# Convolution layer: second weights of the first group and the table transfers put elsewhere

## The chip, the cores and the metric

The kernel runs on one core of a Trainium2 chip. The metric is the device time of one execution in microseconds; the time before is the median of three runs. The profiles are hardware traces of one execution. The engines are PE (matrix products; its weight loads are shown as PEld), DVE (vector operations), ACT (activations and copies), POOL (here almost only an issuer of DMA transfers, among them those that add to what lies at the destination) and SP (issues plain DMA transfers).

## The reference

A decoder trunk of two layers on 512 tokens of width 1024: first an attention layer with a gated MLP, then a convolution layer with a gated MLP. The change concerns the input projection of the convolution layer:

```python
def short_conv_mixer(h, norm_g, w_in, conv_w, w_out):
    xn = rms_norm(h, norm_g)
    proj = xn @ w_in
    gate_b = proj[..., :CONV_WIDTH]
    gate_c = proj[..., CONV_WIDTH:2 * CONV_WIDTH]
    u = proj[..., 2 * CONV_WIDTH:]
    y = gate_b * causal_dwconv(gate_c * u, conv_w)
    return y @ w_out
```

`rms_norm` scales each token by the reciprocal root of its mean square and each channel by a gain. The result is added to `h`, and an MLP follows (`conv_ffn`: up-projection, a convolution of width 3, a SiLU gate, down-projection).

## The kernel before

**Precision.** Each fp32 operand is split into a high and a low part (ACT writes the high part by a copy, L315 and L1029, DVE the rest by a subtraction, L316 and L1031), and a product is taken as three matmuls: high with high, low with high, high with low. Tiles are named accordingly: `whi_p2c` and `wlo_p2c` are the two parts of the weights for the product p2 of the convolution layer (the c at the end), `p_hic` and `p_loc` the parts of its activations.

**Seven products for eight.** The large projections are cut into 2 x 2 blocks (two halves of the width, two halves of the tokens) and computed with seven block products in place of eight, p1, p7, p3, p6, p2, q5 and q4 (class `Sevens`, function `seven`). One product is 24 matmuls of 128 x 256. For a group `g` of columns the weights arrive as blocks X, Y, W and Z by SP's loads; the sums that the products need are made in place: POOL adds a block into Y by a DMA, DVE adds X to Y (L1148, kept in the program as `up.summed`), POOL adds another block into X by a DMA (L1108), DVE adds W to Y (L1203). So p1 takes X, p7 takes Y, p6 takes Y with X added, p2 takes W, q5 takes X with a block added, q4 takes Y with W added, and p3 takes Z. `weights_of` splits one of them; `up.rest` is the low part that it made last. The buffers of the high and low parts rotate, three of each, and SP's loads into W, Z and the plain weights share three buffers as well.

**The convolution layer** (`conv_seven`). The first four tiles of the input projection are plain products (`accs`, 24 matmuls of 128 x 512 each) with the table `plan` that says what is issued at which step (tile, k). Meanwhile the sum of squares is finished, its reciprocal root is turned into a row over the tokens (`norm.row`, tile `nrow`), `row2` is the square of that row, and `gate(o)` scales one of the four tiles by the row and so frees its bank. Then 35 slots follow, seven for each of five groups 0 to 4; slot 7 g + s issues product s of the list above for group g (in place of p3 of the own group, that of the group before). Slot 5 of the last group takes its p3. In slot s == 2, `kept` copies p7's result (`P7s`) on ACT and the weights of p2 are split, if they have not been split before. After it comes the output projection with weights `in_conv_w_out` (L309 loads, split at L315 and L316), whose left operand is `y`, `y_hi` and `y_lo`.

**Tables.** The second MLP uses tables of summed weights (`t`, in device memory), made from `in_ffn_w_up` by DMA steps on POOL (`table_steps`, L114 and L117), each of which moves 768 KB or 1 MB from device memory to device memory. Most are issued during attention; the last seven, of the third table, are issued by `sum_far(99)` in slot 30 of the convolution layer (group 4, s == 2).

**Order.** The program is written in one order, and the framework puts each engine's instructions into a queue by that order and by what is ready in its model; an engine runs its queue in order. `pin` keeps an instruction in program order among the pinned ones of its engine (all of POOL's transfers, and the high parts in `weights_of`). `behind(a, b)` puts a behind b in their engine's queue. `norm.scaled(fn)` calls `fn` as soon as the row has been written in the program, which here is inside `spread`, directly behind the copy of the row on ACT (L397).

Of the kernel before, what the change touches and what calls it, by code (L numbers as in the profile page):

```python
# [17 lines left out]
F32 = mybir.dt.float32  # L18
# [4 lines left out]
ALU = mybir.AluOpType  # L23
AX = mybir.AxisListType

P = 128
# [31 lines left out]
def trunk(  # L58
# [17 lines left out]
    pin = tc.keep_in_program_order  # L76
    act, dve, pe, pool = InOrder(nc.scalar), InOrder(nc.vector), nc.tensor, nc.gpsimd
# [4 lines left out]
    tiny = ctx.enter_context(tc.tile_pool(name="tiny", bufs=4))  # L82
# [7 lines left out]
    def bank(tag):  # L90
        n_ps[0] += 1
        return ps.tile([P, S], F32, tag=tag, name=f"ps{tag}{n_ps[0]}", bufs={"a": 2, "b": 4, "c": 2}[tag])

    def f32(ap):
        return ap.bitcast(F32)
# [120 lines left out]
    def behind(later, earlier):  # L216

        tc.add_manual_dep(
            later.ins, earlier.ins.name,
            mybir.DependencyInfo(mybir.DependencyClass.NoSync, mybir.DependencyReason.DATA), reason="order",  # L220
        )
# [102 lines left out]
    def fetch(n):  # L324
        while len(ready) < min(len(wanted), at[0] + n):
            ready.append(load(len(ready)))
            split_all(len(ready) - 1)
# [209 lines left out]
    gate = const.tile([P, NB, 8], F32, tag="gate", name="gate")  # L537
# [328 lines left out]
    norm = Norm("n0", 0)  # L866
# [110 lines left out]
    def sum_far(n):  # L977
        for _ in range(n):
            next(sums_far, None)
# [26 lines left out]
    norm = Norm("n1", 0)  # L1006
# [365 lines left out]
    def conv_seven(norm, mp, rp):  # L1372
# [5 lines left out]
        up = Sevens("c", mp, range(5), block_of)  # L1378
# [7 lines left out]
        row2 = mp.tile([P, S], F32, tag="row2", name="row2")  # L1386
# [8 lines left out]
        def conv(o, src):  # L1395
            return causal_conv(place(o, 1)[:, 0, :], src, lambda i: conv_tap(i, o))
# [74 lines left out]
        def gate(o, acc):  # L1471
            return dve.tensor_tensor(early_b[:, o, :], acc, norm.row, op=ALU.mult)
# [8 lines left out]
        first = weights()  # L1481
        for f in (0, 1, 4, 5, 2, 3, 6, 7):
            raw.take(f)
        norm.scaled(lambda: dve.tensor_tensor(row2, norm.row, norm.row, op=ALU.mult))
        accs = [bank("b") for _ in range(4)]
        plan = {
            (0, 7): open_first, (1, 0): lambda: (raw.make("p7"), up.weights_of(0, "p1", "X")), (1, 2): lambda: raw.make("p6"),
            (2, 6): lambda: up.first_sums(0), (2, 7): lambda: (gate(0, accs[0]), gate(1, accs[1])), (3, 4): lambda: gate(2, accs[2])}
        for j, acc in enumerate(accs):
            for k, _ in enumerate(products(acc, weights() if j else first, (4, 5, 6, 7, 0, 1, 2, 3))):  # L1490
                if (j, k) in plan:
# [3 lines left out]
        for s in range(35):  # L1495
            up.slot(s // 7, s % 7)
            if s == 0:
                for to, src in zip(kept, up.forms["p1"]):
                    act.activation(to, f32(src), AF.Copy)
                up.forms["p1"] = kept  # L1500
                behind(gate(3, accs[3]), up.rest)
                behind(raw.make("q5"), up.summed)
            if s == 2:
                behind(raw.make("p3"), up.rest)
            if s == 30:
                sum_far(99)
            if s == 34:
                behind(conv(7, wides[3]["yg"][:, 1, :])[0], up.joined)
                fetch(1)
# [200 lines left out]
    with tc.tile_pool(name="mlp0", bufs=1, reuse_waits="tile") as mp:  # L1710
        norm = mlp(0, norm, mp)

    rp = ctx.enter_context(tc.tile_pool(name="rp", bufs=1))
    with tc.tile_pool(name="mix", bufs=1, reuse_waits="tile") as mp:
        ys, place = conv_seven(norm, mp, rp)

    with tc.tile_pool(name="mlp1", bufs=1, reuse_waits="tile") as mp:
        norm = Norm("n3", 8)
        blocks, up = up_begin(1, norm, mp, rp)
# [80 lines left out]
```

## Time and profile before

| What | Value |
|---|---|
| Median of three runs | 1120.63 us (1119.94 to 1121.14) |
| The profiled execution, its own time | 1119.98 us |
| Its span, first to last instruction | 1117.9 us |
| Granted clock of PE | 1.00 |
| Convolution layer, input projection in plain tiles | 609 to 633 us |
| Its five groups | 633 to 736 us |
| Output projection | 736 to 781 us |

A profile's page gives busy time by engine and the costliest groups. The views of the trace used below are: the timeline of one engine (start, duration, engine, line, operation, out<-in, shapes, and in brackets the idle time before it and what ended that), the chain of waits that ended last (start, duration, what), the waits of one engine (engine and line, who was waited for: us in total, times, longest), the DMA view of a window (queues: packets, MB, share of 16 DMA engines; issues: out<-in, KB each, us from issue to landing) and the groups by line. PE's matmuls are pipelined: a row lasts longer than the interval at which they are issued, so lost time on PE is best read from the starts.

### The profile page before, as it was taken

To read this page: it belongs to the slowest core of one execution; us is meant where nothing else is said; L and a number is where in the kernel's file an instruction comes from. 1 tells how busy PE (TensorE), PEld (TensorE's weight loads), DVE (VectorE), ACT (ScalarE), POOL (GpSimd) and SP (SyncE) were. 2 spreads that over 40 slices of the span, in tenths; PEclk is the share of its full clock that TensorE was granted. 3 is DMA by queue.
4 is the path that set the end of the run, shared out by engine and by line. 5 is a ranking of instruction groups with operands and counts; after the bars stand their busy time and mean duration, and the time that the engine had idled before them with its cause. 6 is when DMAs were issued, how large, how long until landed. Compare 5 with 4: busy or idle time off the path is not lost.

```text
span 1117.9 us, 19894 instructions
## 1 busy us (share of the span) xinstructions
PE 1108.3 (99%) x7875; PEld 1015.5 (91%) x7875; DVE 963.3 (86%) x1482; ACT 689.6 (62%) x1020; POOL 180.9 (16%) x205
## 2 busy tenths in 40 slices
PE   9999999999999999999999999999999999999998
PEld 7888787878899999999999899988999999998886
DVE  6798988987899787898989889777889999999886
ACT  7466677655466666676558655445666656667553
POOL 4011111110012221114401001010112221014300
PEclk9999999999999999999999999999999999999999
DMA  6678878689678887899964765696879887899951
GB/s 196 168 182 200 202 167 218 179 213 226 181 175 198 202 208 177 214 276 191 228 174 122 181 169 137 126 261 175 214 173 218 205 200 181 220 260 203 232 153 56
DMA packets 178108, 214.08 MB, mean 192 GB/s; under 512 B 7676, under 2 KB 143916, under 8 KB 178016
## 3 DMA queue, kind: packets, MB, share of 16 engines
q0 software_dynamic: 53280, 95.34, 44.3%
q1 hardware_dynamic: 124576, 117.42, 33.2%
q8 instruction: 61, 1.00, 0.4%
q14 instruction: 31, 0.25, 0.1%
q10 hardware_dynamic: 160, 0.07, 0.0%
HBM read 205.72 MB, written 44.04 MB: 223 GB/s over the span
## 4 chain that ended last, share of the span: by engine, by line
PE 93%; DVE 4%; issue 1%; ACT 1%; DMA 1%; DVEq 0%; ACTq 0%
PE psb L1081 30%; PE psa L1081 12%; PE psb L1677 11%; PE psa L1677 8%; PE psb L336 5%; PE psb L338 5%; PE psb L337 5%; PE psb L712 2%; PE psa L809 2%; PE psa L338 1%; PE psa L337 1%; PE psa L336 1%; PE psc L784 1%; PE psb L594 1%; DMA Xc<-in_conv_w_in 1%
## 5 line engine op out<-in xcount | busy, mean ns | idle before, releaser
L1081 PE MATMUL psb<-p_hi,whi_p 128*128 128x256 f32 x480 | 135.2, 282 | 0.0
L1081 PE MATMUL psb<-p_lo,whi_p 128*128 128x256 f32 x480 | 135.1, 282 | 0.0
L1081 PE MATMUL psb<-p_hi,wlo_p 128*128 128x256 f32 x480 | 135.0, 282 | 0.0
L315 ACT ACTIVATE whi<-raw 128x1024 fp32r<-128x1024 f32 (+2 forms) x77 | 79.0, 1027 | 70.9 <-PE psb L337 22.2
L316 DVE TENSOR_TENSOR wlo<-raw,whi 128x1024 fp32r<-128x1024 f32 (+2 forms) x77 | 90.8, 1180 | 21.7 <-ACT whi L315 21.2
L1081 PEld LDWEIGHTS psb<-p_hi,whi_p 128*128 128x128 f32 x480 | 90.9, 189 | 0.0
L1081 PEld LDWEIGHTS psb<-p_lo,whi_p 128*128 128x128 f32 x480 | 90.4, 188 | 0.0
L1081 PE MATMUL psa<-p_hi,wlo_p 128*128 128x256 f32 x320 | 90.2, 282 | 0.0
L1081 PE MATMUL psa<-p_lo,whi_p 128*128 128x256 f32 x320 | 90.1, 282 | 0.0
L1081 PEld LDWEIGHTS psb<-p_hi,wlo_p 128*128 128x128 f32 x480 | 90.1, 188 | 0.0
L1081 PE MATMUL psb<-q_lo,whi_q 128*128 128x256 f32 x320 | 90.1, 282 | 0.0
L1081 PE MATMUL psb<-q_hi,whi_q 128*128 128x256 f32 x320 | 90.0, 281 | 0.0
L1081 PE MATMUL psb<-q_hi,wlo_q 128*128 128x256 f32 x320 | 90.0, 282 | 0.0
L1081 PE MATMUL psa<-p_hi,whi_p 128*128 128x256 f32 x320 | 89.9, 281 | 0.0
L336 PE MATMUL psb<-hs_a,whi 128*128 128x512 f32 x176 | 72.7, 415 | 0.0
L338 PE MATMUL psb<-hs_a,wlo 128*128 128x512 f32 x176 | 70.0, 398 | 0.0
L1677 PE MATMUL psb<-act,whi 128*128 128x256 f32 x352 | 63.0, 282 | 0.1
L1081 PEld LDWEIGHTS psa<-p_hi,whi_p 128*128 128x128 f32 x320 | 60.7, 190 | 0.1
L1081 PEld LDWEIGHTS psb<-q_hi,whi_q 128*128 128x128 f32 x320 | 60.6, 189 | 0.0
L1081 PEld LDWEIGHTS psa<-p_lo,whi_p 128*128 128x128 f32 x320 | 60.3, 188 | 0.1
L1081 PEld LDWEIGHTS psb<-q_lo,whi_q 128*128 128x128 f32 x320 | 60.3, 188 | 0.0
L1081 PEld LDWEIGHTS psa<-p_hi,wlo_p 128*128 128x128 f32 x320 | 60.1, 188 | 0.0
(553 smaller groups left out, 3658.5 us busy)
## 6 DMA issues: line engine op xcount, KB each, us to landing
t<-in_ffn_w_up POOLq DMA_DIRECT2D x24, 768.0 KB, 8.1
raw<-in_attn_w_in SPq DMA_DIRECT2D x24, 512.0 KB, 5.6
t<-in_ffn_w_up POOLq DMA_DIRECT2D x12, 1024.0 KB, 10.8
X<-in_ffn_w_up SPq DMA_DIRECT2D x20, 512.0 KB, 5.1
Y<-t SPq DMA_DIRECT2D x20, 512.0 KB, 6.7
three<-t SPq DMA_DIRECT2D x20, 512.0 KB, 5.6
W<-in_ffn_w_up SPq DMA_DIRECT2D x20, 512.0 KB, 4.0
Z<-in_ffn_w_up SPq DMA_DIRECT2D x20, 512.0 KB, 5.7
```

Source lines behind the costliest of these rows:

```text
L315: return (act.activation(hi[:, at_], raw[:, at_], AF.Copy), dve.tensor_tensor(lo[:, at_], raw[:, at_], f32(hi[:, at_]), op=ALU.subtract))
L316: dve.tensor_tensor(lo[:, at_], raw[:, at_], f32(hi[:, at_]), op=ALU.subtract))
L336: made = [pe.matmul(acc, w[0], rhs[0], start=first, stop=False), pe.matmul(acc, w[0], rhs[1], start=False, stop=False), pe.matmul(acc, w[1 ...
L337: pe.matmul(acc, w[0], rhs[1], start=False, stop=False),
L338: pe.matmul(acc, w[1], rhs[0], start=False, stop=last)]
L594: pe.matmul(acc, lhs[0], w[0], start=first, stop=False)
L712: pe.matmul(ss[e][:, c:c + wide], ql[rows, b * P:n], kl[rows, 0:wide], start=first and b == bs[0], stop=last and b == bs[-1])
L784: pe.transpose(t[:, k * P:(k + 1) * P], w[:, e, k * P:(k + 1) * P], ident)
L809: pe.matmul(out_, w, t[:, first:first + step * (NB - k - 1) + 1:step, :], start=k == 0 and i == 0, stop=k == NB - 1 and i == 1)
L1081: pe.matmul(to, w[a][:, k, c], x[b][:, k, :], start=fresh and i + k + t == 0, stop=i == 1 and k == 3 and t == 2, skip_group_check=not fresh)
L1677: pe.matmul(to, l, r, start=begin and o + t == 0, stop=end and t == 2 and o == (0 if layer else 1), skip_group_check=not fresh)
```

## The change

Four things are done in `conv_seven`:

- `row2` is no longer issued with the row; it is issued at step (2, 7) of the plan with the first two gates, and all three, and the third gate, stand behind `up.summed`, the addition of X to Y in group 0.
- `up.first_sums(0)` (p7's weights, that addition, and the POOL addition into X) is issued at step (1, 3) in place of (2, 6).
- p2's weights of group 0 are split at the end of slot 1, ahead of the copy `P7s` of slot 2.
- In slot 30 a POOL operation (`hold`, one column, pinned) reads the X of group 4 before the seven table steps are issued, so it waits for the landing of POOL's addition into that X.

```diff
-        norm.scaled(lambda: dve.tensor_tensor(row2, norm.row, norm.row, op=ALU.mult))
         accs = [bank("b") for _ in range(4)]
         plan = {
             (0, 7): open_first, (1, 0): lambda: (raw.make("p7"), up.weights_of(0, "p1", "X")), (1, 2): lambda: raw.make("p6"),
-            (2, 6): lambda: up.first_sums(0), (2, 7): lambda: (gate(0, accs[0]), gate(1, accs[1])), (3, 4): lambda: gate(2, accs[2])}
+            (1, 3): lambda: up.first_sums(0),
+            (2, 7): lambda: [behind(made, up.summed) for made in (
+                dve.tensor_tensor(row2, norm.row, norm.row, op=ALU.mult), gate(0, accs[0]), gate(1, accs[1]))],
+            (3, 4): lambda: behind(gate(2, accs[2]), up.summed)}
...
                 behind(gate(3, accs[3]), up.rest)
                 behind(raw.make("q5"), up.summed)
+            if s == 1:
+                up.weights_of(0, "p2", "W")
             if s == 2:
                 behind(raw.make("p3"), up.rest)
             if s == 30:
+                hold, summed = tiny.tile([P, 1], F32, tag="hold", name="hold", bufs=1), up.st[4]["X"][:, 0, 0:1]
+                pin(pool.tensor_tensor(hold, summed, summed, op=ALU.add))
                 sum_far(99)
```

## The prediction

> **What bounds the kernel now.** I read the page first: the busy shares.
>
> ```profile
> span 1117.9 us, 19894 instructions
> PE 1108.3 (99%) x7875; PEld 1015.5 (91%) x7875; DVE 963.3 (86%) x1482; ACT 689.6 (62%) x1020; POOL 180.9 (16%) x205
> ```
>
> PE bounds nearly everything, so an edit that leaves the matmuls alone can only give back time in which PE stood still. The second view is who PE waited for from 600 to 800 us, the stretch of the convolution layer.
>
> ```profile
> PE psb L1081 <- DVE wlo_q4c L1031: 1.3, 1, 1.3
> PE psb L1081 <- ACT whi_q4c L1029: 0.4, 1, 0.4
> PE psb L1081 <- ACT whi_q5c L1029: 0.3, 1, 0.3
> ```
>
> Nearly all of it is for q5 and q4 weights. These waits undercount, since a matmul's row outlasts its issue interval. The third view, the chain in order of time, gives the price of a product (24 matmuls) and shows two places; PE's timeline gives their edges.
>
> ```profile
> 635.70 2.85 PE psb L1081 x24
> 651.54 2.83 PE psa L1081 x24
> 715.00 8.85 DMA Xc<-in_conv_w_in
> 723.95 1.07 ACT whi_q5c L1029
> ```
>
> ```profile
> 641.23 0.28 PE L1081 MATMUL psa<-p_hic,whi_p2c 128*128 128x256 f32 x1
> ...
> 722.90 0.28 PE L1081 MATMUL psa<-p_hic,whi_p2c 128*128 128x256 f32 x1
> ...
> 736.48 0.39 PE L336 MATMUL psa<-y,whi 128*128 128x512 f32 x1
> ```
>
> **Place A**, group 0: from p2's first matmul to the next group's p1 pass 651.54 - 641.23 = 10.31 us for three products (p2, q5, q4) that need 3 x 2.85 = 8.55. Lost: 1.76 us. **Place B**, group 4: from p2 to the output projection pass 736.48 - 722.90 = 13.58 us for four products, 11.40. Lost: 2.18 us. Together 3.94 us, 0.35% of the time; this is about all that the change can reach.
>
> **The change, part one: group 0's weights (place A).** ACT's and DVE's timelines show why PE waits.
>
> ```profile
> 632.88 1.06 ACT L1029 ACTIVATE whi_p6c<-Yc 128x1024 fp32r<-128x1024 f32 x1 [3.36 <-PE psb L338]
> ...
> 635.74 0.58 ACT L1189 ACTIVATE psb<-psa 128x512 f32<-128x512 f32 x1
> 638.57 0.60 ACT L1143 ACTIVATE P7sc<-psb 128x512 f32<-128x512 f32 x1 [2.25 <-PE psb L1081]
> 639.07 1.05 ACT L1029 ACTIVATE whi_p2c<-Wc 128x1024 fp32r<-128x1024 f32 x1
> ...
> 643.51 1.04 ACT L1029 ACTIVATE whi_q5c<-Xc 128x1024 fp32r<-128x1024 f32 x1
> ```
>
> ```profile
> 628.61 0.69 DVE L1484 TENSOR_TENSOR row<-nrow_n 128x512 f32<-128x512 f32 x1 [0.88 <-ACT nrow_n L397]
> ...
> 631.55 1.21 DVE L1148 TENSOR_TENSOR Yc<-Yc,Xc 128x1024 f32<-128x1024 f32 x1
> ...
> 640.15 1.23 DVE L1031 TENSOR_TENSOR wlo_p2c<-Wc,whi_p2c 128x1024 fp32r<-128x1024 f32 x1 [1.65 <-ACT whi_p2c L1029]
> ...
> 643.64 1.23 DVE L1031 TENSOR_TENSOR p_loc<-early,p_hic 128x1024 fp32r<-128x1024 f32 x1 [1.13 <-ACT p_hic L1029]
> 644.78 1.22 DVE L1031 TENSOR_TENSOR wlo_q5c<-Xc,whi_q5c 128x1024 fp32r<-128x1024 f32 x1
> 645.92 1.22 DVE L1031 TENSOR_TENSOR wlo_q4c<-Yc,whi_q4c 128x1024 fp32r<-128x1024 f32 x1
> ```
>
> ACT runs in order: whi_p2 stands behind the P7s copy, which waits until PE has finished p7, though p2's weights need nothing of it. DVE then idles 1.65 us for whi_p2 and 1.13 us behind it, and its queue ends with wlo_q4 at 645.92 + 1.22 = 647.14.
>
> The call moved to slot 1 puts whi_p2 behind the copy of 635.74 instead, 636.3 to 637.4. Its buffer, the one of p1, is free at 635.70, when p1's product ends. P7s, now behind whi_p2 on ACT, isn't due before 638.55, so it costs nothing (if ACT were late there, at most its 1.05 us). DVE's gap of 1.65 goes, and that of 1.13 if whi_q5 is split ahead of p3's copy: wlo_q5 ends 1.65 to 2.78 us sooner than 646.00, at 644.35 to 643.2, and wlo_q4 at 645.5 to 644.4. PE, unstalled, ends p2 at 644.08 and wants wlo_q5 with its third matmul at 644.3 and wlo_q4 near 647.2. whi_q5 follows p3's copy, itself 1.65 us sooner, and ends near 643; needed 644.08. So 1.76 us come back, with 0 to 1.1 us to spare. What is late next is group 1's p1, due at 649.8 then; its ACT half stands one instruction behind whi_q4 and moves with it.
>
> The other moves of this part carry no gain of their own on PE; a row of PE's timeline tells why.
>
> ```profile
> 626.88 0.40 PE L337 MATMUL psb<-hs_b,whi 128*128 128x512 f32 x1
> ```
>
> p7's weights go in front of the row. They take the buffer of the third projection tile's weights, and at 626.88 PE is on the fourth (its first products read hs_b), so whi_p7 fits ahead of the row's copy, wlo_p7 ends near 629 and the addition Y+X moves from 631.55 to there. POOL's addition into X stands behind Y+X and comes as much sooner. The square of the row and two gates, three operations of 0.69 us, now follow Y+X and end near 632.3; the banks that the gates free are wanted at 635.70. p6's weights gain nothing: they wait for PE (3.36 us above). The cover is over 3 us; without it the three would cost 2.07 at most. On the queues, group 1's addition into Y follows X's on POOL, and SP's next load waits for W's buffer, which wlo_p2 frees; both come sooner and nobody waits for them. Bounds for part one: 0 (the order of the engines stays as it is) to 1.76. I take 1.76.
>
> **Part two: the hold (place B).** POOL's timeline; then the times to landing, of the five POOL additions into X together, and of single transfers from windows that hold one issue (group 2's and group 4's addition, and the load of the first output weight).
>
> ```profile
> 715.00 1.28 POOL L1108 DMA_DIRECT2D Xc<-in_conv_w_in  x1 [16.75 <-issue]
> 715.74 1.50 POOL L114 DMA_DIRECT2D t<-in_ffn_w_up  x1
> ...
> 780.88 1.33 POOL L1108 DMA_DIRECT2D X<-in_ffn_w_up  x1 [11.85 <-DVE wlo_p L1031]
> ```
>
> ```profile
> DMA to landing us min/median/max: 5.7/7.1/8.8
> ...
> Xc<-in_conv_w_in POOLq DMA_DIRECT2D x1, 512.0 KB, 7.4
> ...
> Xc<-in_conv_w_in POOLq DMA_DIRECT2D x1, 512.0 KB, 8.8
> ...
> raw<-in_conv_w_out SPq DMA_DIRECT2D x1, 512.0 KB, 14.0
> ```
>
> ```profile
> q0 software_dynamic: 642, 0.99, 62.7%
> ```
>
> The additions into X take 5.7 to 8.8 us, and the 8.8 is group 4's, the one with a table transfer of 1 MB issued 0.74 us behind it. whi_q5 starts when it lands (723.95). The last row is the software queue, POOL's, from 715 to 724 us: 0.99 MB moved before the 0.5 MB of X had landed. So table bytes ran among those of X.
>
> The hold is one POOL addition on one column of X; POOL, in order, issues the seven left table steps only when X has landed. How long X takes without a table behind it, but with the load of the output weights beside it (14.0 us row), no row shows. Bounds: 5.7 (the fastest of the five) and 8.8 (nothing gained). I take 7.2, next to the 7.4 of group 2, where SP issued a load of the same size right behind X too. That lands X 1.6 us sooner. ACT, DVE and the q4 weights behind it follow one for one, since DVE had been idle before wlo_q5; PE gets 1.6 of its 2.18 us. Bounds in time: 0 to 2.18.
>
> One rule of the Trainium skill speaks against this part: "DMA: Bandwidth & Descriptors", section "Queues, rings and completion order", says that each DMA engine consumes a ring's descriptors in ring order. By it a table issued later on the same ring couldn't hold X up, and part two would give nothing. The 0.99 MB speak against it; whether completion alone is late, no run here shows.
>
> Queued behind the hold are the table steps and then, on POOL, the next layer's first X addition (780.88), ahead of which POOL was idle for 11.85 us. The tables start about 7 us later, so that is covered. The hold itself is nearest to this row, a POOL addition from the groups by line; it lies beside PE's work.
>
> ```profile
> L527 POOL TENSOR_TENSOR by<-two 128x4 f32<-128x4 f32 x1 | 0.7, 717 | 0.1
> ```
>
> **The sum.** The profiled execution took 1119.98 us, its span 1117.9 and 2.1 around it. 1119.98 - 1.76 - 1.6 = 1116.6. The median of the runs is 0.65 above that execution, 1120.63, so the forecast is **1117.2 us**, 0.3% faster.
>
> **The rivals.** A measurement of this kernel can tell about 0.2% (2.24 us) from no change.
>
> *The hold doesn't bring X sooner* (its lateness is that of the load beside it): only 1.76 come back, **1118.9**. For it: the load goes ahead of it in both cases. Against: 7.4 with such a load and no table. 0.15.
>
> *Part one leaves its stall* (another weight is as late, or the order doesn't change): 1.6 come back, **1119.0**. The spare of 0 to 1.1 us at wlo_q5 is the thin place. 0.12. Neither part works: 1120.6, 0.03.
>
> *The delayed tables hit the output weights*, the slower side. The third output weight's time to landing, the two queues from 739 to 744 us, and the timelines of ACT, DVE and PE:
>
> ```profile
> raw<-in_conv_w_out SPq DMA_DIRECT2D x1, 512.0 KB, 4.9
> ```
>
> ```profile
> q0 software_dynamic: 234, 0.94, 102.9%
> q1 hardware_dynamic: 44, 0.02, 1.9%
> ```
>
> ```profile
> 737.62 1.06 ACT L315 ACTIVATE whi<-raw 128x1024 fp32r<-128x1024 f32 x1 [2.86 <-DVE hs_a_conv L1408]
> 738.59 1.04 ACT L1029 ACTIVATE y_hi<-hs_a_conv 128x1024 fp32r<-128x1024 f32 x1
> ...
> 740.44 1.22 DVE L1031 TENSOR_TENSOR y_lo<-hs_a_conv,y_hi 128x1024 fp32r<-128x1024 f32 x1
> ...
> 742.63 0.40 PE L337 MATMUL psa<-y_lo,whi 128*128 128x512 f32 x1
> ```
>
> In those 5 us, with two table transfers running, SP's loads (q1) moved 0.02 MB: tables all but stop them. The third output weight is issued at 732.6 and lands 4.9 us later; on ACT y_hi stands behind its split, y_lo follows on DVE and ends at 741.66, and PE wants it at 742.63: 0.97 us spare. The issue and PE move together, so each us of transit beyond 5.9 costs one. Before, a table step was under way at its issue, and after, one will be too (the steps follow one another), so I expect 5 to 6. At the 14.0 of the first output weight it would cost 8.1: **1125.3**. It turns the sign at 5.9 + 3.4 = 9.3 us. 0.08.
>
> **How the numbers follow.** Forecast 0.62, from 1116.2 (both places empty, and run-to-run spread) to 1118.2 (a us given back at the output weights); nearly all of it is faster by over 0.2%. The two rivals at 1118.9 and 1119.0 and the 1120.6 fall within 0.2%. Faster 0.60, same 0.32, slower 0.08. The range goes from 1116.2 over the two rivals to 1119.6.
>
> **What will show it.** Right: whi_p2 ahead of P7s on ACT in group 0; no waits of PE for q5 or q4 there; POOL's table issue about 7 us behind its X addition; X landing within 7.5 us; a wait for wlo_q4 in group 4 of at most 0.6 us; the output projection starting about 3.4 us sooner. Wrong: X still 8.8 us on its way; an output weight's landing in PE's chain from 735 to 745 us; new waits at the next layer's first products.

## The result and the profile after

| | median | range | executions |
|---|---|---|---|
| before | 1120.29 us | 1119.72 to 1121.14 | 5 |
| after | 1109.76 us | 1106.48 to 1112.01 | 5 |

The ratio is 0.9905, 95% interval 0.9885 to 0.9925: 10.5 us faster, some three times what was forecast (1117.2) and outside the range (1116.2 to 1119.6). The profiled execution after took 1109.76 us, span 1107.4; before it was 1119.98 and 1117.9. One execution of 3809 us, of the hold with the 32 bytes further down, is left out of its row.

First the page after: span, busy shares, and the shares of the chain that ended last. The line under it is the chain of before.

```profile
span 1107.4 us, 19897 instructions
PE 1089.7 (98%) x7875; PEld 992.9 (90%) x7875; DVE 960.1 (87%) x1482; ACT 684.1 (62%) x1020; POOL 181.1 (16%) x206
...
PE 64%; DVE 13%; issue 10%; DMA 10%; ACT 3%; POOL 0%; SPq 0%; DVEq 0%; ACTq 0%; POOLq 0%
```

```profile
PE 93%; DVE 4%; issue 1%; ACT 1%; DMA 1%; DVEq 0%; ACTq 0%
```

The same 7875 matmuls keep PE busy for 18.6 us less (1108.3 before). The change adds and removes no matmul, so many of them must have become cheaper. The chain in order of time says where: three products (72 matmuls of 128 x 256) of the **first** MLP, before and after, start, duration, what.

```profile
439.53 8.52 PE psb L1081 x72
```

```profile
436.58 8.16 PE psb L1081 x72
```

8.52/72 = 118.3 ns, 8.16/72 = 113.3 ns, at a granted clock of 1.00 in both. This is some 170 us ahead of the first instruction that the diff touches. So I compared the starts of the same PE matmuls stage by stage (the length of a stage is the difference of two starts; place A is 10.15 by these, since the chain's row that the prediction took for its end begins 0.16 later):

| Stage | before | after | difference |
|---|---|---|---|
| first MLP, 2436 matmuls of 256 columns | 288.82 | 280.62 | -8.20 |
| place A (group 0: p2, q5, q4) | 10.15 | 9.39 | -0.76 |
| group 1's p1 to group 4's p2 | 71.52 | 70.68 | -0.84 |
| place B (group 4: p2 to the output projection) | 13.57 | 12.99 | -0.58 |
| output projection | 45.01 | 46.54 | +1.53 |
| second MLP, 1848 matmuls of 256 columns | 331.98 | 329.84 | -2.14 |

Most of the gain lies in an MLP that the change doesn't touch. And it is not all that the quicker matmuls offer. Taking the steps in which a 256-wide matmul directly follows another (under 135 ns from start to start), their mean fell from 118.3 to 113.5 ns in the first MLP and from 118.8 to 114.0 in the second: 2435 steps x 4.8 ns = 11.7 us and 1848 x 4.7 = 8.7 us on offer. What the longer steps cost beyond that rose from 0.7 to 4.3 and from 0.6 to 6.9 us: 3.6 and 6.3 given back. PE's waits tell on whom. First the longest of the convolution after (592 to 790 us; engine and line, who was waited for, us in total, times, longest), then those of the second MLP after (from 773 us on). For both MLPs before, this view has no line at all.

```profile
PE psb L1081 <- DVE wlo_q4c L1031: 1.3, 1, 1.3
PE psa L1081 <- ACT whi_p1c L1029: 1.0, 1, 1.0
PE psa L1081 <- DVE wlo_p1c L1031: 0.8, 1, 0.8
PE psa L337 <- DVE y_lo L1031: 0.8, 1, 0.8
```

```profile
PE psb L1081 <- DVE wlo_q L1031: 1.8, 3, 0.8
PE psa L1683 <- DVE wlo L316: 0.5, 1, 0.5
```

The MLP weights' low parts on DVE, which PE didn't wait for in this view at 118 ns a matmul, are late at 113. In the chain DMA has gone from 1 to 10% and DVE from 4 to 13%.

By the stages, place A still loses 9.39 - 3 x 2.72 = 1.23 us and place B 12.99 - 4 x 2.72 = 2.11 (a product of 24 matmuls lasts 2.72 now). The wait in the output projection, from the chain:

```profile
722.97 7.93 DMA raw<-in_conv_w_out
...
731.00 1.06 ACT whi L315
732.06 0.95 ACT y_hi L1029
733.04 0.92 DVE y_lo L1031
```

The third output weight took 7.9 us, with y_hi and y_lo behind its split: the rival of the prediction on the slower side, at 1.5 us. It is a matter of this execution: in the six other profiles with the hold that load took 3.7 to 4.1 us, in the eight without it 4.3 to 5.2, and their output projections lasted 44.8 to 45.2 us.

### The profile page after: what moved, and what is told of

Read it like the earlier page. It is cut to its first block, busy times and chain, and to the rows that moved or that the text cites. A ratio compares the mean times of both kernels' runs of the same rounds, so it can differ in the third digit from the quotient of the medians.

```text
span 1107.4 us, 19897 instructions
## 1 busy us (share of the span) xinstructions
PE 1089.7 (98%) x7875; PEld 992.9 (90%) x7875; DVE 960.1 (87%) x1482; ACT 684.1 (62%) x1020; POOL 181.1 (16%) x206
## 4 chain that ended last, share of the span: by engine, by line
PE 64%; DVE 13%; issue 10%; DMA 10%; ACT 3%; POOL 0%; SPq 0%; DVEq 0%; ACTq 0%; POOLq 0%
PE psb L1081 13%; PE psb L1683 10%; PE psa L1683 7%; PE psa L1081 5%; PE psb L336 5%; PE psb L338 4%; PE psb L337 4%; DMA three<-in_ffn_w_up 4%; DVE wlo_p L1031 3%; PE psb L712 2%; DMA raw<-in_conv_w_out 2%; PE psa L809 2%; DMA Xc<-in_conv_w_in 1%; DMA raw<-in_ffn_w_down 1%; PE psc L784 1%
## 5 line engine op out<-in xcount | busy, mean ns | idle before, releaser
L1081 PE MATMUL psb<-p_hi,whi_p 128*128 128x256 f32 x480 | 132.8, 277 | 0.0
L1081 PE MATMUL psb<-p_lo,whi_p 128*128 128x256 f32 x480 | 132.6, 276 | 0.0
L1081 PE MATMUL psb<-p_hi,wlo_p 128*128 128x256 f32 x480 | 132.5, 276 | 0.0
L1081 PE MATMUL psb<-q_hi,wlo_q 128*128 128x256 f32 x320 | 89.2, 279 | 2.3 <-DVE wlo_q L1031 2.3
L1081 PEld LDWEIGHTS psb<-p_hi,wlo_p 128*128 128x128 f32 x480 | 90.0, 188 | 0.2 <-DVE wlo_p L74 0.2
L1081 PEld LDWEIGHTS psb<-p_lo,whi_p 128*128 128x128 f32 x480 | 90.1, 188 | 0.0
L1081 PEld LDWEIGHTS psb<-p_hi,whi_p 128*128 128x128 f32 x480 | 90.1, 188 | 0.0
L1081 PE MATMUL psa<-p_hi,wlo_p 128*128 128x256 f32 x320 | 89.5, 280 | 0.2
L1081 PE MATMUL psb<-q_hi,whi_q 128*128 128x256 f32 x320 | 88.8, 277 | 0.4 <-ACT whi_q L1029 0.2
L1081 PE MATMUL psb<-q_lo,whi_q 128*128 128x256 f32 x320 | 88.6, 277 | 0.0
L1081 PE MATMUL psa<-p_lo,whi_p 128*128 128x256 f32 x320 | 88.5, 277 | 0.0
L1081 PE MATMUL psa<-p_hi,whi_p 128*128 128x256 f32 x320 | 88.5, 276 | 0.0
L1081 PEld LDWEIGHTS psb<-q_hi,wlo_q 128*128 128x128 f32 x320 | 60.0, 188 | 3.3 <-DVE wlo_q L1031 3.1
L1081 PEld LDWEIGHTS psa<-p_hi,wlo_p 128*128 128x128 f32 x320 | 60.0, 188 | 1.4 <-DVE wlo_p L1031 0.7
L1081 PEld LDWEIGHTS psb<-q_hi,whi_q 128*128 128x128 f32 x320 | 60.1, 188 | 0.7 <-ACT whi_q L1029 0.4
L1081 PEld LDWEIGHTS psa<-p_hi,whi_p 128*128 128x128 f32 x320 | 60.1, 188 | 0.1
L1081 PEld LDWEIGHTS psa<-p_lo,whi_p 128*128 128x128 f32 x320 | 60.1, 188 | 0.1
```

The costliest lines, as they stand in the source:

```text
L1081: pe.matmul(to, w[a][:, k, c], x[b][:, k, :], start=fresh and i + k + t == 0, stop=i == 1 and k == 3 and t == 2, skip_group_check=not fresh)
```

## The experiments

**The idea.** `hold` is a new tile of 4 bytes a partition in the pool `tiny`. It takes 32 bytes, and every tile allocated behind that pool, among them all moving operands of L1081 and of the MLPs' second products, starts 32 bytes higher. Theory A: this shift is the gain. Theory B: the moved steps are. Theory C: a state of the chip. Below, D is the start of the stationary operand (weights) less that of the moving operand, in bytes, modulo 128. Within one kernel all weight tiles have one remainder modulo 128, and all moving tiles of L1081 have one (but for the 24 matmuls of group 0's p1, which read hs_a and have D at 0), so D is one number.

**The shift alone**, the change without the shift, and the change shifted twice as far.

```diff
     warm = tiny.tile([P, 1], F32, tag="warm", name="warm", bufs=1)
+    tiny.tile([P, 1], F32, tag="pad", name="pad", bufs=1)
```

> The kernel before, with its order of instructions untouched; one tile of 4 bytes a partition (32 with padding) is allocated next to the tile of the first activation and never used, so that every tile allocated behind that pool starts 32 bytes higher, as it does after the change. Theory A (addresses: the shift alone made the 256-wide matmuls of L1081 and L1677 quicker, from 118.6 to 113.8 ns from start to start): 113 to 114 ns from the first MLP on, and 1110 to 1114 us, that is what the change gave less up to 3.4 us for its two parts. Theory B (the moved steps made the matmuls quicker): 118.6 ns and 1120 us. Theory C (a state of the chip in those runs): no tie to the kernel, 1120 or 1110 alike for all kernels of this job.

```diff
-                hold, summed = tiny.tile([P, 1], F32, tag="hold", name="hold", bufs=1), up.st[4]["X"][:, 0, 0:1]
+                hold, summed = warm, up.st[4]["X"][:, 0, 0:1]
```

> The whole change, but the hold writes into the tile of the first activation, dead since the first microseconds, so that nothing is allocated and all addresses are those of before. Theory A: 118.6 ns at L1081 and the forecast of the prediction, 1116.2 to 1118.2 us with 1117.2 the likeliest. Theory B: 113.8 ns and 1110 us. Theory C: as the other kernels of this job.

The 64-byte kernel is the change with the line of the first diff added.

> The whole change with one more unused tile, so that the tiles behind the pool stand 64 bytes higher than before instead of 32. Theory A with a period of 64 bytes: 118.6 ns again and about 1117 us; theory A with a period of 128 bytes: an interval of its own, 118.6 or near it if only one of four positions is quick. Theory B: 113.8 ns and 1110 us.

**The other places.** Taking `warm` out of `tiny` lowers the tiles by 32 bytes:

```diff
-    warm = tiny.tile([P, 1], F32, tag="warm", name="warm", bufs=1)
+    warm = xin.tile([P, 1], F32, tag="warm", name="warm", bufs=1)
```

> The kernel before with the tile of the first activation taken out of the small pool, so that the tiles behind it start 32 bytes lower (the moving operand of L1081 32 bytes past a multiple of 128, as its stationary one: D of 0 modulo 128). Theory A2: 119 to 121 ns, like the 23 matmuls with hs_a as moving operand, which stand at D of 0 in all kernels so far (119.1 ns), and 1120 to 1128 us. Rival, a period of 64 bytes: 113.8 ns and 1112 us.

A first tile in `const` moves all tiles together; with the pad in `tiny` besides, the moving operands go 32 bytes further than the weights:

```diff
     const = ctx.enter_context(tc.tile_pool(name="const", bufs=1))
+    const.tile([P, 1], F32, tag="pad0", name="pad0")
```

> The kernel before with an unused tile of 32 bytes ahead of all others, so that every tile moves by 32 bytes together: the moving tiles stand where they stand after the change, the weights 32 bytes higher too (difference of the starts 96 modulo 128, as before). If the difference decides: 118.3 to 118.8 ns and 1119 to 1122 us. If the place of the moving operand decides: 113.4 to 113.9 ns and 1110 to 1112 us.

> As e13 with a second unused tile in the small pool: weights 32 bytes higher, moving tiles 64 bytes higher, where they stood in the kernel at 1125 us, and the difference of the starts 64 modulo 128, as after the change. If the difference decides: 113.4 to 113.9 ns and 1110 to 1113 us. If the place of the moving operand decides: 119.5 ns and 1122 to 1126 us.

Measured (starts modulo 128 from the addresses that the tiles were given; mean step from start to start of the directly following 256-wide matmuls):

| Kernel | weights | moving | D | step, ns | median, us | ratio to before |
|---|---|---|---|---|---|---|
| before | 32 | 64 | 96 | 118.5 | 1120.29 | |
| the change | 32 | 96 | 64 | 113.8 | 1109.76 | 0.9905 [0.9885, 0.9925] |
| shift alone | 32 | 96 | 64 | 113.9 | 1112.12 | 0.9922 [0.9905, 0.9938] |
| change, no shift | 32 | 64 | 96 | 118.7 | 1121.37 | 1.0009 [0.9998, 1.0019] |
| change, 64 bytes | 32 | 0 | 32 | 119.5 | 1125.17 | 1.0045 [1.0030, 1.0060] |
| 32 bytes less | 32 | 32 | 0 | 118.8 | 1118.85 (one execution) | |
| all moved by 32 | 64 | 96 | 96 | 118.5 | 1121.11 | 1.0004 [0.9994, 1.0014] |
| weights 32, moving 64 | 64 | 0 | 64 | 113.8 | 1112.73 | 0.9932 [0.9919, 0.9945] |

The chain's rows for 72 matmuls of the first MLP say the same, in the order shift alone, change without shift, 64 bytes, all moved by 32, weights 32 and moving 64 (a line added ahead of it in the code makes L1081 L1082 or L1083):

```profile
455.94 8.16 PE psb L1082 x72
```

```profile
439.89 8.55 PE psb L1081 x72
```

```profile
439.75 8.61 PE psb L1082 x72
```

```profile
439.69 8.52 PE psb L1082 x72
```

```profile
475.70 8.16 PE psb L1083 x72
```

What follows: the shift alone makes the kernel faster, with not one instruction moved, and without the shift the whole change has no gain to be measured. Theory B and theory C fall. The last two rows settle what counts: with the moving tiles at their addresses of after, but the weights moved along, the step is 118.5; with the moving tiles where the slow 64-byte kernel has them, and D at 64, it is 113.8. In the layer it is the difference of the two starts, not the place of either. The kernel at D of 0 came out quicker than was expected (118.8 ns and 1118.85 us in one execution, for 119 to 121 and 1120 to 1128). Of the four remainders only 64 is quick.

**Bare series.** The layer's matmuls have company, so I ran series of them alone. In the first chart, the starts of moving and stationary operand go in steps of 32 bytes:

> Not the layer: 43 series of 56 matmuls of 256 columns (fp32r, 128x128 stationary), parted by four of 128 columns, with the start of the moving operand at 0, 32, 64 or 96 bytes past a multiple of 128 and the start of the stationary operand likewise, 16 pairs, and eleven pairs off these steps; the 16 pairs once on an otherwise quiet core and once beside additions on DVE and copies on ACT. Theory A, if the starts modulo 128 are all that counts: moving 96 with stationary 32 gives 113 to 114 ns, moving 64 or 32 with stationary 32 gives 118 to 120 ns, in one or both of the passes. Theory A, if the place of the stationary operand counts too, shows it in the other rows. If every pair has one interval, it is not the starts modulo 128 alone. Theories B and C: one interval for all.

Mean step of each series, ns, its slow first step with it (rows: start of the stationary operand; columns: of the moving one):

| | 0 | 32 | 64 | 96 |
|---|---|---|---|---|
| 0 | 120.8 | 118.8 | 118.7 | 120.8 |
| 32 | 119.3 | 120.7 | 118.7 | 118.8 |
| 64 | 114.6 | 119.2 | 120.8 | 117.5 |
| 96 | 119.8 | 114.5 | 119.2 | 120.7 |

DVE's additions ran beside the first eight series of the first pass, ACT's copies beside the first of the second, which repeats the first pass within 0.1 ns. Two of the four pairs with D at 64 are quick, and the pair of the layer (moving 96, stationary 32) is not: theory A as I had it, with each start by itself, didn't foretell the layer from the chart. The second chart takes the order of L1081:

> Not the layer: 59 series of matmuls in the order of L1081 (four tiles of 128 rows, each with hi by hi, hi by lo and lo by hi, two column halves), the starts set by D = start of the stationary operand less start of the moving one, in bytes. 256 columns at D of 0 to 480 in steps of 32, at -32 to -128, at 64 with both moved together by 4, 16, 32, 64, 96, 256 and 512 bytes, and at 48, 60, 68 and 80; 512 columns at D of 0 to 480; and 256 columns in the order of the first chart, for D of 0 to 224 and -32 to -128. Theory A2 (D modulo 128 alone decides, 64 is quick): 113 to 115 ns at D of 64, 192, 320, 448 and -64 and 118 to 121 ns at the others, the same for all places at D of 64. Theory A3 (each start by itself decides): the places at D of 64 differ among each other. Rival: no series below 118 ns in this order, so that what made L1081 quick isn't in the starts of these operands. For 512 columns no theory says anything; 227 ns at the quick ones and 232 at the others would be the like.

With the moving start at 0, D at 64 and 320 gave 114.4, D at 192 and 448 gave 118.6, and the twelve others 118.6 to 120.6. With D at 64 and the pair moved together, 16, 64, 96 and 512 bytes gave 114.4 to 114.6, but 32 and 256 gave 118.5 and 4 bytes 121.8. D of 48, 60, 68 and 80 gave 119.0 to 120.3, and the order of the first chart, run again for twelve values of D, the same as that of L1081 within 0.1 ns. So D modulo 128 alone (A2) fell too, and so did a rule for the starts modulo 128, since moving both by 256 bytes changed the step; that the place of the pair counts (A3) was still open. The slow ones at D of 64 modulo 128 had something in common: nearly all their steps were 117 to 119 ns, where most other D gave 115 to 125. That looked like a second steady pace. So the third chart puts different work in front of the same series:

> Not the layer: series of 72 matmuls of 256 columns in the order of L1081, each behind one of six lead-ins (four or five of 128 columns, three of 128 and one of 192 or of 144, two of 512, four of 256), for the pairs of starts (moving, stationary) of (0, 64), (0, 192), (512, 448), (32, 96), (256, 320) and (0, 0) bytes; three long series of 288; and three series in which the starts change on the way. Theory A4 (a pair of starts whose difference is 64 modulo 128 has two steady paces, 114.4 and 118.6 ns, and the work ahead decides which one it falls into): the first five pairs show either of the two by lead-in, (0, 0) always 120.6 ns, and a quick stretch stays quick when the difference changes from 64 to 192. Theory A3 (the pair alone decides): each pair has one pace behind all lead-ins, and the pace changes with the pair inside a series.

Behind two matmuls of 512 columns (L76), the pair (0, 64) in L147 and (0, 192) in L150; behind four of 256, the same pairs in L165 and L168 (PE's timeline; 72 matmuls between a start and the next row of L76):

```profile
188.73 0.28 PE L147 MATMUL acc<-mh,wh 128*128 128x256 f32 x1
...
196.90 0.62 PE L76 MATMUL wide<-mh,wh 128*128 128x512 f32 x2
197.36 0.28 PE L150 MATMUL acc<-mh,wh 128*128 128x256 f32 x1
...
205.84 0.64 PE L76 MATMUL wide<-mh,wh 128*128 128x512 f32 x2
...
241.63 0.28 PE L165 MATMUL acc<-mh,wh 128*128 128x256 f32 x1
...
250.11 0.64 PE L76 MATMUL wide<-mh,wh 128*128 128x256 f32 x4
250.59 0.28 PE L168 MATMUL acc<-mh,wh 128*128 128x256 f32 x1
...
258.75 0.64 PE L76 MATMUL wide<-mh,wh 128*128 128x256 f32 x4
```

(0, 64): 8.17/72 = 113.5 ns behind one lead-in, 8.48/72 = 117.8 behind the other. (The pairs are written as start of the moving and of the stationary operand, and from here on D is the whole difference, not its remainder.) (0, 192): 8.48/72 = 117.8 and 8.16/72 = 113.3, the other way round. All five pairs with D of 64 modulo 128 show both 113.3 and 117.8 in their steady part, behind one lead-in or another; (0, 0) shows 120.0 behind all six. The lead-in alone doesn't decide either: behind four matmuls of 128 columns the pair (0, 64) ran at 117.8 in two series (L93, L210) and at 113.3 in two (L201, L226). And a pace can outlive a change of the starts. One series has 48 matmuls each of D 64 (L210), 192 (L212), 64 (L214) and 192 (L216); another of D 64 (L226), 0 (L228), 64 (L230) and two more:

```profile
454.25 0.28 PE L212 MATMUL acc<-mh,wh 128*128 128x256 f32 x1
...
459.90 0.28 PE L214 MATMUL acc<-mh,wh 128*128 128x256 f32 x1
...
465.34 0.28 PE L216 MATMUL acc<-mh,wh 128*128 128x256 f32 x1
...
470.78 0.56 PE L76 MATMUL wide<-mh,wh 128*128 128x128 f32 x4
```

```profile
493.67 0.28 PE L228 MATMUL acc<-mh,wh 128*128 128x256 f32 x1
...
499.42 0.28 PE L230 MATMUL acc<-mh,wh 128*128 128x256 f32 x1
...
505.08 0.28 PE L232 MATMUL acc<-mh,wh 128*128 128x256 f32 x1
```

L212, at D 192, runs at 5.65/48 = 117.7; L216, at the same D, at 5.44/48 = 113.3, with L214 in the quick pace (5.44/48) ahead of it. So both paces outlived the change from 64 to 192 (the slow one from L210, at 117.8 in its steady part, to L212), while the change from 192 to 64 turned the slow one into the quick one (L212 to L214, and again in a third series, L219 to L221). L226 started at 488.16 and is quick after its first steps (5.51/48 = 114.8), D of 0 takes 5.75/48 = 119.8, and behind it the same D of 64 runs at 5.66/48 = 117.9. Of theory A4 this much is shown: D of 64 modulo 128 makes a quick pace possible, and the pair alone doesn't decide whether it is taken, so A3 falls. That the work ahead does is the likely reading, but how far back it reaches isn't shown, and each order was run in one execution. In the layer all seven profiles with D at 64 averaged 113.8 to 114.0. The slow pace turns up there too, and passes: in the second profile of the change, PE lost 2.8 us at group 4's p1, and the products behind it took 2.85, 2.85, 2.75 and then 2.72 us again. What in the chip makes the two paces isn't shown.

**The two parts of the change at the addresses of before.** Part one is the change without the two lines of the hold; the hold alone is the kernel before with them, writing into `warm`.

> Part one alone at the addresses of before. By the prediction's step: 1.76 us come back at the first group, 1118.9 us beside 1120.6. By what the unshifted change showed (place A lost 0.63 us instead of 1.76): 1.0 us come back, 1119.5. Rival: nothing to be measured, 1120.5, since runs of one kernel differ by more.

> The hold alone at the addresses of before, written into the dead tile of the first activation. By the prediction's step: X lands 7.2 us after its issue and 1.6 us come back, 1119.0 us. By what the unshifted change showed (X lands in 7.8 us, and q4's lo weight stands behind four operations of the gates on DVE and ACT): 0.5 to 1 us, 1119.7. Rival (the tables hit the third output weight in most runs): 1121 to 1122, with a wait of PE for y_lo of 0.5 us or more.

> The change without its shift once more, beside its two parts on one chip. By the sum of the prediction: 1117.2 us. By the first ten runs: 1121.4. Theory: its two parts give 1.5 us in the convolution, as the first profile of it shows, and what takes them back in the other runs is seen in this profile if it falls into the slower of them: a wait of PE for y_lo in the output projection, or the first MLP, whose code is the one of before.

Medians, ratios, and stages from the profiles (us):

| | before | part one | hold | both |
|---|---|---|---|---|
| median | 1120.0 | 1119.63 | 1122.2 | 1121.41 |
| ratio | | 0.9999 [0.9988, 1.0009] | 1.0017 [1.0008, 1.0026] | 1.0005 [0.9995, 1.0014] |
| first MLP | 288.82 | 288.85 | 288.81 | 289.79 |
| place A | 10.15 | 9.16 | 10.15 | 9.16 |
| group 1's p1 to group 4's p2 | 71.52 | 72.04 | 71.64 | 71.69 |
| place B | 13.57 | 12.88 | 12.45 | 12.67 |
| these three together | 95.24 | 94.08 | 94.24 | 93.52 |
| transit of group 4's X, a part of them | 8.85 | 8.15 | 7.73 | 7.95 |
| output projection | 45.01 | 45.00 | 45.02 | 45.24 |
| second MLP | 331.98 | 331.98 | 332.07 | 334.08 |

Part one gives 1.0 us at place A, as the main theory of these runs said, and half of it goes at group 4's p1, where PE comes 1.15 us sooner and ACT's half of the weights only 0.6 (708.67 us for 709.29). PE's waits in the convolution, part one alone:

```profile
PE psb L1081 <- DVE wlo_q4c L1031: 1.2, 1, 1.2
PE psa L1081 <- DVE wlo_p1c L1031: 0.5, 1, 0.5
PE psb L1081 <- DVE wlo_q5c L1031: 0.4, 1, 0.4
```

The convolution's end hangs on group 4's X. ACT and DVE at place B, before and after the change with its shift:

```profile
723.95 1.06 ACT L1029 ACTIVATE whi_q5c<-Xc 128x1024 fp32r<-128x1024 f32 x1 [5.00 <-DMA Xc<-in_conv_w_in]
729.64 1.22 DVE L1031 TENSOR_TENSOR wlo_q4c<-Yc,whi_q4c 128x1024 fp32r<-128x1024 f32 x1
```

```profile
714.28 1.06 ACT L1029 ACTIVATE whi_q5c<-Xc 128x1024 fp32r<-128x1024 f32 x1 [4.33 <-DMA Xc<-in_conv_w_in]
719.99 1.22 DVE L1031 TENSOR_TENSOR wlo_q4c<-Yc,whi_q4c 128x1024 fp32r<-128x1024 f32 x1
```

In all fifteen profiles of the layer whi_q5 starts 0.1 us after X has landed, wlo_q4 5.7 us after that, and the output projection 12.5 us after whi_q5 (12.3 with D at 64). So place B shrinks when X lands sooner, and also when PE comes to it later. X's transit varies with and without the hold; the kernel with 32 bytes less, which has no hold, has 7.8 us and a place B of 12.53. With the transit taken off, the three stages together last 86.4 to 86.6 us in the four profiles without part one at D of 96 or 0, the hold alone among them, and 85.6 to 86.0 in the three with it. So part one is worth 0.4 to 1.0 us there, and the hold nothing.

The hold alone makes the kernel slower, by the medians. In its own profile it isn't seen to cost anything (that execution, at 1120.09, is one of the quicker ones of eleven; eight of them took 1121.8 to 1123.1). The profile of both shows a cost that fits. ACT, the split of the seventh output weight, before and with both parts; then that load's time to landing:

```profile
760.88 1.06 ACT L315 ACTIVATE whi<-raw 128x1024 fp32r<-128x1024 f32 x1 [5.08 <-DMA raw<-in_conv_w_out]
```

```profile
762.98 1.06 ACT L315 ACTIVATE whi<-raw 128x1024 fp32r<-128x1024 f32 x1 [7.16 <-DMA raw<-in_conv_w_out]
```

```profile
raw<-in_conv_w_out SPq DMA_DIRECT2D x1, 512.0 KB, 14.7
```

It was 11.8 us before. A table step is issued 2.7 us behind it, where before one was issued 0.4 us ahead of it; that the later tables are the cause is my reading. ACT and DVE stay 2.1 us behind from there, and PE meets that at the start of the second MLP (its waits from 776 to 790 us, both parts):

```profile
PE psc L410 <- DVE nacc_n L74: 0.8, 1, 0.8
PE psa L1081 <- DVE wlo_p L1031: 0.8, 1, 0.8
```

That this is what the slower executions of the hold alone have as well is argued, not shown: none of them was profiled, and in four of the seven profiles with the hold this load took 8.7 to 8.8 us, in the others 12.5 to 14.7. What the hold does bring is the loads ahead: the second output weight, which without the hold is on its way beside the first table step and with it mostly ahead of that step, took 9.2 to 10.5 us in the eight profiles without the hold and 3.7 to 5.5 in the seven with it. PE wasn't waiting for it.

The first MLP of both took 1.0 us longer than before, with the code and the addresses of before: 8.55 against 8.52 for 72 matmuls in the rows above. So at D of 96 too there are two paces, here 118.3 and 118.8 ns (the second MLP ran at 118.8 in all six profiles with D at 96), and what decides isn't shown. Both profiles of this kernel, the change without its shift, have 118.8 in the first MLP, and the four of other kernels 118.3: the instructions up to there are the same, but two executions can't exclude a tie to the kernel. It may be a part of the 2 to 4 us by which executions of one kernel differ.

**The parts at the quick pace.** The same with the 32 bytes:

> Part one of the change (second weights of the first group ahead of the row, row and gates behind the sum), no hold, and the 32 bytes. Main theory: part one gives the 1.0 us at the first group that it gave without the shift (place A lost 1.76 us before and 0.63 us in the unshifted change), and the output weights stay as in the shifted kernel: 1111 us, 0.1% below the shifted kernel alone. Rival 1, the forecast's price: 1110.3. Rival 2, nothing at all: 1112.

> The hold alone, without part one, with the 32 bytes. Main theory: what the hold gives at group 4 (about 1 us) is given back at the output projection, where PE waits for y_lo behind the third output weight: a wait of 1 to 1.5 us for y_lo, and 1112 us, as the shifted kernel alone. Rival 1 (the hold gives its 1.6 us and nothing is given back): 1110.5. Rival 2 (delayed tables cost more later): over 1113.

> Part one with the 32 bytes, no hold. If the hold costs at the quick pace what it costs at the old one (0.17%, about 1.9 us): 1108.5 to 1110 us, 1 to 2 us below e16. If hold and part one are both worth nothing there: as e16 and as the shift alone, 1110 to 1112.

> The change as it is, on the chip of e15. First runs of it: 1109.76, a ratio of 0.9905 [0.9885, 0.9925]. The same here; against e15 as told there.

| | median, us | ratio to before |
|---|---|---|
| part one, first time | 1109.78 | 0.9910 [0.9880, 0.9940] |
| hold | 1111.25 | 0.9901 [0.9873, 0.9928] |
| part one, second time | 1108.88 | 0.9903 [0.9888, 0.9918] |
| the change, second time | 1112.69 | 0.9935 [0.9917, 0.9954] |

Side by side on one chip, part one alone was 3.8 us below the whole change, as expected if the hold costs; but the intervals touch, the first time the change had 0.9905, and the hold alone 0.9901. The version with part one and 32 unused bytes is the fastest median seen (1108.88), and against the change that lead isn't settled. In the second profile of the change place B took 11.23 us, against 12.99 in the first. That is no gain of the hold: the stretch ahead of it, from group 1's p1, took 72.75 for 70.68, since PE lost 2.8 us at group 4's p1 where it had lost 1.2, and the output projection started, as in the first, 12.3 us after whi_q5. With X's transit taken off, the three stages last 85.1 to 85.5 us in the four profiles with part one and 85.9 to 86.3 in the three without, the hold alone at 85.9: the profiles say the same here as at the old pace. The wait of 1 to 1.5 us for y_lo that was expected of the hold alone isn't in its profile, where the output projection took 45.10 us; the first profile of the change (46.54) is the only one that has it.

## Why the prediction was wrong

*"An edit that leaves the matmuls alone can only give back time in which PE stood still"*, 3.94 us in all. **This is the step that failed.** It took the step of 118 ns as given. The edit left the matmuls alone, and moved their operands: 32 bytes of `hold` changed D from 96 to 64, and the shift alone is worth 0.78% (0.9922), nearly all of the 0.95% measured. The line was in the diff, and the prediction priced the hold as one POOL operation and not as a tile. That the kernel came out faster, as forecast, is luck: what made it faster is none of the things that the forecast was added up from.

*Part one, 1.76 us of 0 to 1.76.* The order came out as foretold: whi_p2 goes ahead of P7s, and DVE's gap of 1.65 us is gone. The size was off: 0.99 us at place A (10.15 to 9.16), where 1.60 was there to win (10.15 less 3 x 2.85), not 1.76. The spare of 0 to 1.1 us at wlo_q5 was none. DVE's timeline with part one alone:

```profile
642.25 1.22 DVE L1031 TENSOR_TENSOR p_loc<-early,p_hic 128x1024 fp32r<-128x1024 f32 x1 [1.13 <-ACT p_hic L1029]
643.39 1.22 DVE L1031 TENSOR_TENSOR wlo_q5c<-Xc,whi_q5c 128x1024 fp32r<-128x1024 f32 x1
```

The second gap, of 1.13 us, stayed: p3's copy is still ahead of whi_q5 on ACT. wlo_q5 ended at 644.61, behind the 644.35 that the prediction had as its late end, and PE's q5 took 3.47 us for 2.85: 0.6 lost. What came back was half spent at group 4's p1, whose weights stand behind work that waits for group 3's X and came only 0.6 us sooner; and the convolution's end follows group 4's X, not place A. So adding the two parts up was wrong too. In the medians part one can't be told from nothing (0.9999, 0.9988 to 1.0009, an interval that holds a gain of 1.0 us as well).

*Part two, X in 7.2 us, 1.6 back.* Wrong at the landing, and the rival with 0.15 was right: the hold doesn't bring X sooner. Group 4's X takes 7.8 to 8.8 us (median 8.1) in the eight profiles without the hold and 7.7 to 9.3 (median 8.0) in the seven with it. Here two, the hold alone and part one alone:

```profile
Xc<-in_conv_w_in POOLq DMA_DIRECT2D x1, 512.0 KB, 7.7
```

```profile
Xc<-in_conv_w_in POOLq DMA_DIRECT2D x1, 512.0 KB, 8.2
```

The 8.8 that I read as the table's doing was the upper end of a spread. The rule of the Trainium skill ("DMA: Bandwidth & Descriptors", section "Queues, rings and completion order") that a ring's descriptors are taken in ring order, which stands there among what it says of SP's and ACT's queues, agrees with these landings on POOL's; the 0.99 MB that I held against it don't say whose bytes they were in time. Why X takes 8 us here and 5.5 to 6.2 in groups 0 and 3, with the hold or without, stays open: the load beside it, which the rival names, was in every run. The rest of the step held: the q4 weights and the output projection follow X's landing one for one, 5.7 and 12.5 us after whi_q5.

*The delayed tables hit the output weights, 0.08.* They do in some executions, at two places. At the third weight in the first profile after: 7.9 us of transit, 2.0 beyond the 5.9 that the prediction allowed, and 1.5 us longer in the output projection; the six other profiles with the hold don't have it. At the seventh, a place that it didn't name, with both parts: 14.7 us and 2.1 at the next layer's first products, which it did name as a wrong sign. At the addresses of before the hold alone is 0.17% slower, so this side won; by which of these loads, its profile doesn't show.

So with the addresses held, the forecast of 3.4 us would have been wrong as well: the two parts together are at 1.0009 and 1.0005, and their intervals leave no more than 0.6 us of gain.

## What to carry to other kernels

A new tile, even one of 4 bytes, moves every tile behind its pool. Before reading a gain as that of the edit, compare the matmuls' steps in a stage that the edit doesn't reach, and time two more kernels: the edit without the allocation and the allocation without the edit. Where PE bounds, the start of the moving operands against that of the weights is a free parameter to try in steps of 32 bytes; and when the matmuls get quicker, look at what then ends last, since here 10 of the 20 us on offer in the two MLPs went into new waits, most of those that the view of PE's waits names for DVE. And before adding up two gains of one stage, look for the event that its end follows; here it was the landing of one transfer, 12.4 to 12.7 us ahead of the end in every profile.

## What the runs showed of the hardware

- The step of back-to-back fp32r matmuls of 256 columns was 113.3 to 120.0 ns in its steady part, by the starts of the two operands in steps of 32 bytes, at a granted clock of 1.00 (0.997 to 0.998 in the charts). With D of 64 modulo 128 there are two steady paces, 113.3 and 117.8 ns; D of 0 gave 120.0 in the charts and 118.8 in the layer. "TensorE: Matmul & The Clock Gate" of the Trainium skill, section "Back-to-back issue gap", gives for the gap of a single matmul, without the budget of the weight loads, a formula by which the estimate is 256/2.4 + 2.5 = 109.2 ns; the quickest seen here, with a weight load for each matmul, is 4 ns above that.
- A pace was kept when D changed from 64 to 192 (L210 to L212 slow, L214 to L216 quick), the slow one turned quick when it changed back (L212 to L214), and the quick one was lost over a stretch at D of 0 (L226 to L230).
- At 512 columns, in the second chart, D of 0 and 256 gave 228.4 and 228.7 ns, D of 192 and 448 230.3, and the other twelve 233.3 to 235.3: the D that is quick at 256 columns (64: 234.4) is a slow one there. Each was run once, so a second pace at 512 columns isn't excluded.
- A start 4 bytes off the steps of 16 gave 121.8 ns at D of 64 (second chart).
- A load of 512 KB on SP's queue beside a table step of 1 MB on POOL's took 9.2 to 10.5 us, and 3.7 to 5.5 when most of it ran ahead of the step (the second output weight, without and with the hold). An addition on POOL's queue with such a step issued 0.7 us behind it on the same queue took no longer (7.8 to 8.8 us, and 7.7 to 9.3 without one).
